# Hybrid attention block: stationary q and k weights, a product on GpSimd and later value matmuls in the stick-breaking groups

## Chip, cores, metric

One core of a Trainium2 chip. The metric is the time of one execution on the device in microseconds; the kernel before has a median of 2731.22 us over 3 runs (2727.44 to 2734.09). The profile is of one further execution, 2740.3 us.

## The reference

Sequence 2048, width 1024, one layer; all in float32.

```python
u = rms_norm(h, norm1_w)
dq, dk, dv, sq, sk, sv = split(u @ w_in)
# A: differential attention, 4 heads: two softmax maps per head, T5 bias, chunk-causal
attn = softmax(q0 k0 + bias) - lam * softmax(q1 k1 + bias);  y_A = rms_norm(attn @ v)
# B: stick-breaking attention, 8 heads of 64, strictly causal
z = einsum('bqhd,bkhd->bhqk', q, k) * scale
log_1mb = where(mask, log_sigmoid(-z), 0)
rem = cumsum(log_1mb, reverse=True) - log_1mb
a = where(mask, exp(log_sigmoid(z) + rem), 0);  y_B = rms_norm(a @ v)
h = h + concat(y_A, y_B) @ w_out
h = h + (silu(u2 @ w_gate) * (u2 @ w_up)) @ w_down      # u2 = rms_norm(h, norm2_w)
```

Part B is computed without logarithms: `a` is the sigmoid of z times the running product, from the right, of the sigmoids of -z.

## The kernel before

**Precision.** TensorE multiplies float16. Each operand is split into a high and a low half, and a product is made of three (or all four) of the half products.

**Groups.** The attention runs in 8 groups `g`: groups 0 to 3 are one differential head each (`diff_attn`), 4 to 7 are two stick-breaking heads each (`sb_attn`, head index `m`). A group has three parts.

- *Projection* (`proj`, 16 token tiles of 128). `proj_tile` (L320) keeps a tile of u, 128 x 128, in the array and streams 384 weight columns (q, k, v) past it, 24 matmuls per tile, into one of two PSUM buffers `pj` (pool `psj`). `proj_out` splits q, k into the staging tile `st` and v into `v` (`split_psum`, L327 to L330: the high half by ACT or DVE as `pick` finds by a running load account, the low half by DVE). After four tiles `proj_batch` has SP transpose q and k by DMA (L372) and swap the halves of q by two copies (L374). The tiles of u are loaded for every group (L386). The projection of a group is issued during the group before.
- *Scores to weights* (`stage_a`). For each block of 128 queries `i`, each block `b` of 1024 keys from the right and each head `m`, chunks of up to 512 keys: two score matmuls (L448) into one of four PSUM buffers `sc`; ACT takes sigmoid(-z) to the tile `om` (L554) and sigmoid(z) in place (L555); DVE scans `om` with a running product (L557) and multiplies (L558) into `be`. `be` and `om` are `z4` tiles, 9 buffers. Then `split_t`: ACT casts `be` to float16 (L89) into an `s16` tile (3 buffers), POOL subtracts for the low half (L98), SP transposes the pair by DMA into `aT` (L403, 6 buffers).
- *Values* (`stage_b`, L458): `aT` is the stationary operand, v streams, three matmuls of 64 columns per 128 keys, into the PSUM tile `yp`. It runs `PD` = 5 items behind `stage_a`; at the end of a group a loop drains the rest. After four query blocks `finish` normalises, transposes and stores to `ms`.

`diff_attn` has the same build with softmax (L483 to L507) and with values two query blocks behind.

**Order.** The program is issued once per item and a scheduler orders the instructions of each engine ahead of time on a modelled timeline, by priority and readiness; on the chip every engine takes its queue in that order. During group 7 the output projection (L761) begins; then follows the feed-forward part, where TensorE is busy nearly throughout.

Of the kernel before, what the change touches and what calls it, by code (L numbers as in the profile page):

```python
# [11 lines left out]
F32 = mybir.dt.float32  # L12
# [47 lines left out]
def block(tc, a, out):  # L60
# [3 lines left out]
    with top:  # L64
# [62 lines left out]
        DVE.memset(mhalf[:], -0.5)  # L127

# [122 lines left out]
        with ExitStack() as ph1:  # L251
# [71 lines left out]

            def split_psum(hi, lo, src, n):
# [21 lines left out]

            @pri("pb")
            def proj_batch(g, G, B):
                st, v, raw = B
                qT = sp.tile([P, 4, 4, P], F16, tag="qT", bufs=QB, name=nm("qT"))  # L350
                kT = sp.tile([P, 2, 4, P], F16, tag="kT", bufs=KB, name=nm("kT"))
# [27 lines left out]
            def proj(g, G, fresh=None):  # L379
                for t in range(NT):  # L380
# [6 lines left out]
                    if t % 4 == 0:  # L387
                        st = pp.tile([P, 4, 4, 2, 64], F16, tag="st", name=nm("st"))
                        v = sp.tile([P, 4, 256], F16, tag="v", bufs=KB, name=nm("v"))
                        raw = pp.tile([P, 4, 256], F32, tag="raw", name=nm("raw")) if g < 4 else None  # L390
# [7 lines left out]
            def split_t(src, n, he="ADP", le="DP"):  # L398
                s16 = s16p.tile([P, 2048], F16, tag="s16", bufs=SB, name=nm("s16"))
                to16(s16[:, :n], src, n, he)  # L400
                tt(s16[:, n : 2 * n], src, s16[:, :n], ALU.subtract, n, le)
                aT = sp.tile([P, 16, P], F16, tag="aT", bufs=AB, name=nm("aT"))
# [37 lines left out]

            def fq(g, i):
                k = 2 if g == NG - 1 else 4
                return (i % k, k)

            @pri("sc")
            def score_chunk(G, sc, i, q, m, w, cut=False):
                for o in range(2):
                    PE.matmul(sc[:, : 128 * w].rearrange("p (t n) -> p t n", n=P), lhsT=G["q"][i // 4][:, 2 - 2 * o + m, i % 4, :], rhs=G["k"][q][:, m, 0:w, :], start=o == 0, stop=o == 1)  # L448
                if cut:
                    PE.matmul(sc[:, 128 * w - P : 128 * w], lhsT=idb[:], rhs=tri[:], start=False, stop=True, skip_group_check=True)  # L450
# [9 lines left out]
            def diff_attn(g, G):  # L460
                @pri("at")
                def probs(i):
# [8 lines left out]
                    for m in range(2):  # L471
                        nx = 0
                        for b in range(nb):
                            n = min(1024, L - 1024 * b)
                            z = z4()
                            for c in range((n + 511) // 512):
                                lo, hi = 512 * c, min(512 * c + 512, n)
                                sc = ps.tile([P, 512], F32, tag="sc", bufs=4, name=nm("sc"))
                                score_chunk(G, sc, i, 2 * b + c, m, (hi - lo) // P)
# [35 lines left out]
                def values(i, aTs, ssum):  # L515
                    r, k = fq(g, i)
# [8 lines left out]
                held = []  # L525
                for i in range(NT):
                    if i % 4 == 0:
                        level()
                    held.append((i, probs(i), sums[0]))
                    if len(held) > 2:  # L530
                        values(*held.pop(0))
                    yield ((i + 1) * (i + 2) / 2 + CD * (i + 1)) / (136 + 16 * CD), i + 1
                for u in held:
                    values(*u)

            def sb_attn(g, G):
                last = {}

# [689 lines left out]
```

## Time and profile before

| | |
|---|---|
| median of 3 runs | 2731.22 us |
| profiled execution | 2740.3 us |
| its span, first to last instruction | 2738.5 us |
| busy, share of the span: PE, DVE, POOL, ACT | 91%, 72%, 52%, 49% |
| mean granted TensorE clock | 0.967 |
| first scan of group 4, of group 5, of group 6, of group 7 | 606, 794, 965, 1127 us |

The row of a window gives the busy time of each engine in that stretch. A row of a group of instructions gives line, engine, operation, tiles with their shapes and the count; then busy time in us and the mean of one in ns; then the idle time of the engine in front of them and what ended most of it. Durations of matmuls overlap one another, since the array is pipelined: what a matmul costs in a dense stream is read from the difference of two bursts, not from the mean.

### The profile page before, as it was taken

What the parts mean: (1) busy time and instruction counts of PE and PEld (TensorE: products, weight loads), DVE (VectorE), ACT (ScalarE), POOL (GpSimd) and SP (SyncE); (2) the same over time, 40 slices, a digit from 0 to 9 for tenths busy, and PEclk for the clock granted to TensorE, in tenths of its full rate; (3) what the DMA queues carried; (4) which work ended last, traced back from release to release, by engine and by line L of the source; (5) the groups of instructions that cost most, each with busy time, mean ns of one, the idle gap of its engine ahead of it and who ended that gap; (6) DMA issues with size and microseconds to landing.
All of it is one profiled execution on the core that took longest, in us unless ns stands there. A gap on an engine that the chain in (4) does not pass through costs nothing.

```text
span 2738.5 us, 45414 instructions
## 1 busy us (share of the span) xinstructions
PE 2490.0 (91%) x17084; PEld 1409.8 (51%) x17084; DVE 1978.5 (72%) x3752; ACT 1353.3 (49%) x2539; POOL 1429.8 (52%) x1002
## 2 busy tenths in 40 slices
PE   7998989898978886889989898999999999999999
PEld 4655656565545553457775444444444444444444
DVE  6888879888888989987766777777786544434434
ACT  4665656566868778765644534344342212121121
POOL 2577677765554545546655566565664332222322
PEclk9999999998999997899999999999999999999999
DMA  6788787789998997997896665566657845635532
GB/s 227 199 164 178 151 198 164 180 171 200 208 201 184 212 186 151 203 192 208 213 289 256 220 234 191 208 221 216 231 204 283 316 158 181 220 128 193 192 116 93
DMA packets 646830, 543.52 MB, mean 198 GB/s; under 512 B 506369, under 2 KB 573953, under 8 KB 636369
## 3 DMA queue, kind: packets, MB, share of 16 engines
q1 hardware_dynamic: 644784, 538.53, 71.8%
q8 instruction: 134, 2.20, 0.3%
q0 software_dynamic: 512, 1.36, 0.2%
q10 hardware_dynamic: 1312, 0.72, 0.1%
q14 instruction: 88, 0.71, 0.1%
HBM read 261.08 MB, written 147.32 MB: 149 GB/s over the span
## 4 chain that ended last, share of the span: by engine, by line
PE 36%; DVE 9%; DMA 4%; POOL 3%; issue 3%; ACT 2%; SPq 0%; DVEq 0%; POOLq 0%; ACTq 0%
PE pd L1034 14%; PE pm L934 7%; PE pd L934 5%; PE pa L934 5%; DVE wd L215 2%; PE po L761 2%; DMA stages<-in_w_down_dram 1%; POOL stages L98 1%; DVE wu L215 1%; DMA aT<-s 1%; DVE z L557 1%; DVE cg L999 1%; DVE cg L98 1%; POOL s L98 1%; PE pj L320 1%
## 5 line engine op out<-in xcount | busy, mean ns | idle before, releaser
L98 POOL TENSOR_TENSOR s<-z,s 128x1024 f16<-128x1024 f32 (+7 forms) x288 | 474.4, 1655 | 320.1 <-ACT s L89 281.4
L320 PE MATMUL pj<-w,xt 128*128 128x384 f16 x3072 | 577.0, 336 | 19.2 <-DMA xt<-xs 5.6
L320 PEld LDWEIGHTS <-xt 128*128 128x128 f16 x3072 | 301.5, 101 | 233.1 <-issue 36.1
L557 DVE TENSOR_TENSOR_SCAN z<-z,sc 128x512 f32<-128x512 f32 (+3 forms) x320 | 356.1, 1114 | 72.1 <-ACT sc L555 68.8
L448 PE MATMUL sc<-kT,qT 128*128 128x512 f16 (+3 forms) x1280 | 348.3, 364 | 59.4 <-DVE z L558 23.7
L1034 PE MATMUL pd<-wd,act 128*128 128x512 f16 x1764 | 394.0, 381 | 7.2 <-DVE cu L968 7.1
L458 PE MATMUL yp<-v,aT 128*128 128x64 f16 (+1 forms) x4896 | 281.5, 209 | 82.3 <-DMA aT<-s 81.7
L458 PEld LDWEIGHTS <-aT 128*128 128x128 f16 x4896 | 245.4, 102 | 172.1 <-DMA aT<-s 110.4
L934 PEld LDWEIGHTS <-wg 128*128 128x128 f16 x1848 | 181.8, 98 | 228.1 <-issue 14.6
L934 PEld LDWEIGHTS <-wu 128*128 128x128 f16 x1848 | 180.8, 98 | 216.5 <-issue 2.0
L98 POOL TENSOR_TENSOR act<-cg,act 128x512 f16<-128x512 f32 x109 | 149.8, 1385 | 262.3 <-ACT act L993 262.3
L1034 PEld LDWEIGHTS <-act 128*128 128x128 f16 x1764 | 173.0, 98 | 216.6 <-issue 10.2
L89 ACT CAST s<-z 128x128 f16<-128x128 f32 (+7 forms) x216 | 170.3, 790 | 154.8 <-DMA aT<-s 72.9
L98 POOL TENSOR_TENSOR stages<-stages 128x512 f32<-128x512 f32 x97 | 172.9, 1783 | 120.1 <-DVE wg L215 41.4
L98 POOL TENSOR_TENSOR hs<-hs,cu 128x512 f32<-128x512 f32 x102 | 132.6, 1306 | 165.6 <-DVE hs L1040 62.7
L554 ACT ACTIVATE z<-sc,c 128x512 f32<-128x512 f32 (+3 forms) x320 | 204.4, 639 | 23.7 <-PE sc L448 18.9
L558 DVE TENSOR_TENSOR z<-sc,z 128x512 f32<-128x512 f32 (+3 forms) x320 | 193.7, 606 | 8.5
L555 ACT ACTIVATE sc<-sc,c 128x512 f32<-128x512 f32 (+3 forms) x320 | 196.5, 614 | 0.0
L1040 DVE SCALAR_TENSOR_TENSOR hs<-pd,c,hs 128x512 f32<-128x512 f32 x144 | 106.5, 748 | 118.5 <-PE pd L1034 113.6
L761 PE MATMUL po<-wo,mt 128*128 128x256 f16 x1536 | 180.7, 275 | 12.3 <-DVE xf L764 6.8
L993 ACT CAST act<-cg 128x512 f16<-128x512 f32 x126 | 76.9, 616 | 231.4 <-DVE cg L999 192.7
L934 PE MATMUL pm<-X,wu 128*128 128x512 f16 x792 | 179.1, 379 | 1.8 <-ACT cg L979 1.7
(241 smaller groups left out, 4109.1 us busy)
## 6 DMA issues: line engine op xcount, KB each, us to landing
xt<-xs SPq DMA_DIRECT2D x112, 512.0 KB, 4.4
hs<-hd SPq DMA_DIRECT2D x72, 512.0 KB, 4.5
hd<-hs SPq DMA_DIRECT2D x56, 512.0 KB, 5.8
split<-wg SPq DMA_DIRECT2D x11, 1792.0 KB, 6.9
split<-wu SPq DMA_DIRECT2D x11, 1792.0 KB, 6.7
split<-wd SPq DMA_DIRECT2D x11, 1792.0 KB, 6.8
wg<-split SPq DMA_DIRECT2D x11, 1792.0 KB, 7.4
wd<-split SPq DMA_DIRECT2D x11, 1792.0 KB, 9.1
```

What stands on the lines that cost most here:

```text
L89: ACT.copy(dst, src)
L98: (DVE if e == "D" else POOL).tensor_tensor(dst, a_, b_, op)
L320: PE.matmul(pj[:, :384], lhsT=xv[:, xi, kt, :], rhs=G["w"][:, wi, kt, :], start=n == 0, stop=n == 23)
L448: PE.matmul(sc[:, : 128 * w].rearrange("p (t n) -> p t n", n=P), lhsT=G["q"][i // 4][:, 2 - 2 * o + m, i % 4, :], rhs=G["k"][q][:, m, 0:w, ...
L458: PE.matmul(yp[:, y0 : y0 + wd], lhsT=aT[:, a_, :], rhs=v[:, v_ : v_ + wd], start=start and j == 0 and q == 0, stop=stop and j == nb - 1 a ...
L554: ACT.activation(om[:, lo:hi], sc[:, :w], AF.Sigmoid, scale=G["nkz"][:])
L555: ACT.activation(sc[:, :w], sc[:, :w], AF.Sigmoid, scale=G["kz"][:])
L557: DVE.tensor_tensor_scan(ov, ov, sc[:, :w], om[:, hi : hi + 1], op0=ALU.mult, op1=ALU.bypass)
L558: DVE.tensor_tensor(be[:, lo:hi], sc[:, :w], om[:, lo + 1 : hi + 1], ALU.mult)
L761: PE.matmul(po[:, sl], lhsT=mt[:, kt, P * xi : P * xi + P], rhs=wos[2 * h + n][wi][:, kt, :], start=q == 0, stop=q == 23)
L934: PE.matmul(ps_[:].rearrange("p (t n) -> p t n", n=P), lhsT=wv[:, wo, wi, 128 * kt : 128 * kt + 128], rhs=X[xo][:, :, xi, kt, :], start=st ...
L1034: PE.matmul(po[:], lhsT=act[:, ao, xi, 128 * j : 128 * j + 128], rhs=W["d"][:, wo, wi, :], start=start and u == 0 and q == 0, stop=u == nu ...
```

## The change

`turned(g)` holds for groups 4, 5 and 6. In these the weights of q and k are the stationary operand and 128 tokens stream, so q and k come out of PSUM already transposed; v is computed as before, 128 columns at a time. Two tiles share two PSUM buffers, one for q and k, one for v. The transposes and swaps by DMA fall away. q is stored per head, with the other head's 64 rows set to zero by a mask (`half`), and scores take three matmuls: high x high, low x high, high x low. Of each item's chunks those with c = 1 ("aside") write the second sigmoid to SBUF, and their product is POOL's.

For all groups, value matmuls are ordered on PE behind the last score matmul issued before them (`issue_after`), and one list `late` carries pending values from one group to the next. In groups 4 and 5 values run 7 items behind in place of 5, and two further buffers each for `s16` and `aT` come from tiles that lie idle there (`raw`, `st`).

```diff
+            def turned(g):
+                return 4 <= g < NG - 1
+
+            @pri("pm")
+            def proj_turned(G, xt, pq, pv, r):
+                xv = xt[:].rearrange("p (s k n) -> p s k n", s=2, k=KT)
+                for c in range(3):
+                    n = 0
+                    for kt in range(KT):
+                        for xi, wi in ((0, 0), (0, 1), (1, 0)):
+                            w_, x_ = G["w"][:, wi, kt, 128 * c : 128 * c + 128], xv[:, xi, kt, :]
+                            o = pv[:, P * r : P * r + P] if c == 2 else pq[:, 256 * c + P * r : 256 * c + P * r + P]
+                            PE.matmul(o, lhsT=x_ if c == 2 else w_, rhs=w_ if c == 2 else x_, start=n == 0, stop=n == 23)
+                            n += 1
+
+            @pri("po")
+            def turned_out(pq, pv, qT, kT, v, j):
+                two = slice(j - 1, j + 1)
+                q2, k2 = (pq[:, 256 * c : 256 * c + 256].rearrange("p (t n) -> p t n", t=2) for c in range(2))
+                for m in range(2):
+                    ACT.mul(qT[:, m, two, :], q2, half[:, m : m + 1])
+                    DVE.scalar_tensor_tensor(qT[:, 2 + m, two, :], q2, half[:, m : m + 1], qT[:, m, two, :], op0=ALU.mult, op1=ALU.subtract)
+                note("A", 800)
+                note("D", 800)
+                split_psum(kT[:, 0, two, :], kT[:, 1, two, :], k2, 256)
+                vv = v[:, two, :].rearrange("p t (h s e) -> p t h s e", h=2, s=2)
+                split_psum(vv[:, :, :, 0, :], vv[:, :, :, 1, :], pv[:, :256].rearrange("p (t h e) -> p t h e", t=2, h=2), 256)
...
+                    if turned(g):
...
+                        if t % 2 == 0:
+                            pq, pv_ = (psj.tile([P, 512], F32, tag="pj", name=nm("pj")) for _ in range(2))
+                        proj_turned(G, xt, pq, pv_, t % 2)
+                        if t % 2 == 1:
+                            turned_out(pq, pv_, qT, kT, v, t % 4)
...
-            def split_t(src, n, he="ADP", le="DP"):
-                s16 = s16p.tile([P, 2048], F16, tag="s16", bufs=SB, name=nm("s16"))
+            def split_t(src, n, he="ADP", le="DP", wide=None):
+                if wide is not None and wide % 5 in (1, 3):
+                    s16 = pp.tile([P, 4, 256], F32, tag="raw", name=nm("s16"))[:].rearrange("p t n -> p (t n)").bitcast(F16)
+                else:
+                    s16 = s16p.tile([P, 2048], F16, tag="s16", bufs=SB, name=nm("s16"))
...
+                if wide is not None and wide % 4 == 3:
+                    aT = pp.tile([P, 4, 4, 2, 64], F16, tag="st", name=nm("aT"))[:].rearrange("p c t s e -> p (c t) (s e)")
...
+            front, late = [], []
+
+            def behind(n):
+                while len(late) > n:
+                    late.pop(0)()
...
-            def score_chunk(G, sc, i, q, m, w, cut=False):
-                for o in range(2):
-                    PE.matmul(sc[:, : 128 * w].rearrange("p (t n) -> p t n", n=P), lhsT=G["q"][i // 4][:, 2 - 2 * o + m, i % 4, :], rhs=G["k"][q][:, m, 0:w, :], start=o == 0, stop=o == 1)
+            def score_chunk(G, sc, i, q, m, w, cut=False, turned=False):
+                terms = ((m, 0), (2 + m, 0), (m, 1)) if turned else ((2 + m, m), (m, m))
+                for o, (a_, b_) in enumerate(terms):
+                    last = PE.matmul(sc[:, : 128 * w].rearrange("p (t n) -> p t n", n=P), lhsT=G["q"][i // 4][:, a_, i % 4, :], rhs=G["k"][q][:, b_, 0:w, :], start=o == 0, stop=o == len(terms) - 1)
...
                 def values(i, aTs, ssum):
+                    with tc.issue_after(front[-1]):
+                        values_now(i, aTs, ssum)
...
+                    late.append(functools.partial(values, i, probs(i), sums[0]))
+                    behind(2)
...
+                lag = PD + 2 if g < NG - 2 else PD
...
-                        score_chunk(G, sc, i, 2 * b + c, m, w // P, b == i // 8 and hi == n)
+                        front.append(score_chunk(G, sc, i, 2 * b + c, m, w // P, b == i // 8 and hi == n, turned(g)))
+                        aside = c == 1 and turned(g)
+                        beta = be[:, lo:hi] if aside else sc[:, :w]
                         ACT.activation(om[:, lo:hi], sc[:, :w], AF.Sigmoid, scale=G["nkz"][:])
-                        ACT.activation(sc[:, :w], sc[:, :w], AF.Sigmoid, scale=G["kz"][:])
+                        ACT.activation(beta, sc[:, :w], AF.Sigmoid, scale=G["kz"][:])
                         ov = om[:, lo:hi][:, ::-1]
                         DVE.tensor_tensor_scan(ov, ov, sc[:, :w], om[:, hi : hi + 1], op0=ALU.mult, op1=ALU.bypass)
-                        DVE.tensor_tensor(be[:, lo:hi], sc[:, :w], om[:, lo + 1 : hi + 1], ALU.mult)
+                        (POOL if aside else DVE).tensor_tensor(be[:, lo:hi], beta, om[:, lo + 1 : hi + 1], ALU.mult)
...
+                            late.append(functools.partial(stage_b, i, m, b, n, aT))
+                            behind(lag)
...
-                for u in pend:
-                    stage_b(*u)
+                if g == NG - 1:
+                    behind(0)
```

50 lines of the change are left out of this document (32 added, 18 removed).

## The prediction

> **What bounds the kernel now.** I read the stages first: busy time per engine between the first scan of one group and the first scan of the next (columns: window, length, PE, PEld, DVE, ACT, POOL busy, granted clock, DMA share, GB/s). Groups 4, 5 and 6 are the windows that begin at 605, 794 and 965; 150:600 is three of the differential groups, 470:605 the last of them, 1127:1384 group 7.
>
> ```profile
> span 2738.5 us, 45414 instructions
> ...
> 150.00:600.00 450.00, 407.66 (x3279) 263.15 (x3280) 388.89 (x1142) 270.30 (x707) 322.14 (x226) 0.98 0.80 172
> ...
> 470.00:605.00 135.00, 121.40 (x974) 77.91 (x972) 118.83 (x345) 79.78 (x208) 90.96 (x66) 0.97 0.78 169
> 605.00:794.00 189.00, 162.97 (x1614) 103.51 (x1612) 167.12 (x313) 147.21 (x289) 103.03 (x63) 0.94 1.02 207
> 794.00:965.00 171.00, 140.20 (x1420) 86.83 (x1418) 151.78 (x268) 133.61 (x252) 86.20 (x54) 0.91 0.99 195
> 965.00:1127.00 162.00, 123.71 (x1299) 76.04 (x1296) 149.52 (x251) 131.17 (x246) 83.86 (x55) 0.85 0.87 173
> 1127.00:1384.00 257.00, 223.72 (x2289) 172.01 (x2290) 199.51 (x344) 166.08 (x308) 144.96 (x103) 0.96 0.87 205
> ```
>
> Groups 4 to 6 take 522 us. DVE is busy for 468 of them (90%), ACT for 412 (79%), POOL for 273 (52%). DVE leads; its idle time is 54 us. Next, the groups of instructions in 605:1127, and who waited for whom there:
>
> ```profile
> L557 DVE TENSOR_TENSOR_SCAN z<-z,sc 128x512 f32<-128x512 f32 (+3 forms) x240 | 266.9, 1113 | 40.6 <-ACT sc L555 38.0
> L98 POOL TENSOR_TENSOR s<-z,s 128x1024 f16<-128x1024 f32 (+7 forms) x147 | 237.8, 1625 | 229.8 <-ACT s L89 217.1 <-issue 6.3 <-DVE st L330 3.4
> L320 PE MATMUL pj<-w,xt 128*128 128x384 f16 x1166 | 220.2, 339 | 5.4 <-DMA xt<-xs 2.8 <-DVE st L330 1.9 <-DVE m L178 0.7
> L554 ACT ACTIVATE z<-sc,c 128x512 f32<-128x512 f32 (+3 forms) x241 | 153.4, 636 | 14.8 <-PE sc L448 10.2 <-PE sc L450 2.8 <-POOL s L98 1.7
> L555 ACT ACTIVATE sc<-sc,c 128x512 f32<-128x512 f32 (+3 forms) x241 | 147.3, 611 | 0.0
> L558 DVE TENSOR_TENSOR z<-sc,z 128x512 f32<-128x512 f32 (+3 forms) x240 | 145.2, 607 | 6.6
> L448 PE MATMUL sc<-kT,qT 128*128 128x512 f16 (+3 forms) x482 | 139.8, 379 | 42.4 <-DVE z L558 18.3 <-DVE z L545 13.6 <-DVE z L547 8.7
> L458 PE MATMUL yp<-v,aT 128*128 128x64 f16 (+1 forms) x2524 | 123.5, 204 | 45.0 <-DMA aT<-s 44.8
> L89 ACT CAST s<-z 128x1024 f16<-128x1024 f32 (+7 forms) x144 | 115.8, 805 | 77.8 <-DMA aT<-s 44.0 <-DVE z L558 11.7 <-issue 11.5
> ...
> L330 DVE SCALAR_TENSOR_TENSOR st<-pj,st 128x256 f16<-128x256 f32 x49 | 19.8, 407 | 2.1 <-ACT st L327 2.1
> ...
> L327 ACT ACTIVATE st<-pj 128x256 f16<-128x256 f32 x49 | 19.1, 396 | 10.5 <-DVE v L330 10.5
> L327 ACT ACTIVATE v<-pj 128x128 f16<-128x128 f32 x49 | 14.2, 297 | 1.2 <-PE pj L320 1.1
> L330 DVE SCALAR_TENSOR_TENSOR v<-pj,v 128x128 f16<-128x128 f32 x49 | 13.1, 273 | 0.1
> L215 DVE SCALAR_TENSOR_TENSOR w<-wst,sW,w 128x1536 f16<-128x1536 f32 x6 | 12.6, 2110 | 0.0
> ```
>
> The scan and the product behind it are 412 of DVE's 468 us. Of DVE's idle time 38 us are waits of the scan for ACT. ACT in turn lost 44 us in front of its cast (L89): the cast needs a free s16 buffer, which a transposing DMA still reads. The timeline at the seam of groups 4 and 5 shows the chain: ACT stands 2.5 us and 2.0 us at casts, the sigmoids queue behind, and DVE's scan comes 4.55 us late:
>
> ```profile
> 798.95 0.30 ACT L89 CAST s<-z 128x128 f16<-128x128 f32 x1 [2.52 <-DMA aT<-s]
> ...
> 801.25 0.30 ACT L89 CAST s<-z 128x128 f16<-128x128 f32 x1 [2.00 <-DMA aT<-s]
> ...
> 802.29 0.75 DVE L557 TENSOR_TENSOR_SCAN z<-z,sc 128x256 f32<-128x256 f32 x1 [4.55 <-ACT sc L555]
> ```
>
> PE's own 45 us of waits for aT cost little by themselves: the scores wait for DVE as well (42 us), so PE has room.
>
> **The product on GpSimd.** A group has 32 chunks with c = 1 (in i from 4 to 15, both heads), 96 in all: 60 of 512 columns, 12 each of 384, 256 and 128, together 39,936 columns. From the start of a product to the next scan:
>
> ```profile
> 1101.92 0.69 DVE L558 TENSOR_TENSOR z<-sc,z 128x512 f32<-128x512 f32 x1
> ...
> 1102.53 1.27 DVE L557 TENSOR_TENSOR_SCAN z<-z,sc 128x512 f32<-128x512 f32 x1
> ```
>
> That is 0.61 us per 512 columns, so DVE is rid of 39,936/512 x 0.61 = 48 us. POOL's price for a float32 product in SBUF isn't in this stage. The nearest rows, of the whole trace:
>
> ```profile
> L98 POOL TENSOR_TENSOR stages<-stages 128x512 f32<-128x512 f32 x97 | 172.9, 1783 | 120.1 <-DVE wg L215 41.4 <-DVE wd L215 34.1 <-DVE wu L215 31.0
> L98 POOL TENSOR_TENSOR hs<-hs,cu 128x512 f32<-128x512 f32 x102 | 132.6, 1306 | 165.6 <-DVE hs L1040 62.7 <-DVE cu L1040 45.4 <-issue 44.8
> ```
>
> The first is strided, the second contiguous like ours, so I take 1.31 us (bounds 1.31 and 1.78): 78 x 1.31 = 102 us, POOL 273 to 375. ACT writes the second sigmoid to SBUF (636 ns against 611): 96 x 0.025 = 2 us.
>
> Row L215 reads two SBUF operands on DVE and takes 2110 ns. [...]
>
> **The projection.** Before, two token tiles cost DVE 2 x (407 + 273) ns and ACT 2 x (396 + 297). After, the pair has four high halves and four low ones of 256 columns; the lows are DVE's, two highs (q) are ACT's, and of the 48 highs for k and v the compiled order gives DVE 35. DVE: 4 x 0.407 + 35/24 x 0.40 = 2.21 against 1.36, so +0.85 us a pair, 24 pairs, +20 us. A group's projection runs during the group before: 7 us fall into group 3, 14 into groups 4 and 5. ACT gains some 0.4 us a pair.
>
> PE's pitch, from differences of bursts in the timeline, and from a dense stretch of the last phase (234 matmuls of 512 in 50 us):
>
> ```profile
> 66.72 3.58 PE L320 MATMUL pj<-w,xt 128*128 128x384 f16 x21
> ...
> 79.74 1.63 PE L320 MATMUL pj<-w,xt 128*128 128x384 f16 x9
> ...
> 167.07 0.94 PE L458 MATMUL yp<-v,aT 128*128 128x128 f16 x14
> ...
> 168.84 0.67 PE L458 MATMUL yp<-v,aT 128*128 128x128 f16 x9
> ...
> 2150.00:2200.00 50.00, 50.00 (x234) 22.62 (x233) 23.79 (x33) 9.36 (x15) 13.10 (x10) 1.00 0.70 262
> ```
>
> 384 columns: (3.58 - 1.63)/12 = 163 ns. 128 columns with a weight load each: (0.94 - 0.67)/5 = 54 ns, three of them 162. The projection costs PE nothing more. The bursts' raw quotient is 74 ns, the upper bound.
>
> **The scores.** A third matmul per chunk: 240 chunks of 435 columns on average, 435/512 x 0.214 = 0.182 us each, +44 us for PE. What PE can carry beside a busy DVE is seen in the differential groups (150:600, PE alone):
>
> ```profile
> L320 PE MATMUL pj<-w,xt 128*128 128x384 f16 x1225 | 225.2, 328 | 6.2 <-ACT raw L341 5.0 <-DMA xt<-xs 1.1
> L448 PE MATMUL sc<-kT,qT 128*128 128x512 f16 (+3 forms) x560 | 146.5, 356 | 8.8 <-DVE z L483 3.2 <-DVE mx L487 1.8 <-DMA kT<-st 1.5
> L458 PE MATMUL yp<-v,aT 128*128 128x128 f16 x1434 | 114.7, 224 | 25.4 <-DMA aT<-s 25.3
> ```
>
> By pitches that is 1225 x 0.163 + 560 x 0.182 + 1434 x 0.054 = 379 us in 450, 84%, with DVE at 86% and POOL at 72%. In groups 4 to 6 it is 1166 x 0.163 + 482 x 0.182 + 2524 x 0.027 (the 512 pitch scaled to 64) = 346 us, 66% of 522 (more at the granted clock of 0.85 to 0.94). With 390 in 488 us it would be 80%: near the other stage's share, below it. The scores run up to four PSUM buffers ahead of DVE, which covers a late one.
>
> **Transposes, buffers, order.** The 16 transposes and 16 half swaps of groups 5 and 6 leave the queue of SP, and 8 of each of group 4 before it:
>
> ```profile
> L372 SPq DMA_TRANSPOSE qT<-st x32: 1232/1266/2467, 71.7 to 1207.6; - x32
> ...
> L374 SPq DMA_DIRECT2D qT<-qT x64: 467/586/1172, 75.8 to 1216.8; - x64
> ```
>
> That is 24 x 1.27 + 24 x 0.59 = 45 us of issue less in the queue that also issues the aT transposes; worth nothing by itself, it makes s16 free sooner. Two more s16 and two more aT buffers (groups 4 and 5) aim at the 44 us of casts. Values behind later scores is an order within PE's queue: behind a value wait projections and later values, and the aT buffer is released later. In the compiled order a value stands 13 chunks behind its scores in groups 4 and 5 (before 9.5), 10 in group 6 (9), 9 in group 7 (7), and as before in groups 0 to 3, so I expect PE's 45 us of aT waits nearly gone and nothing there for the differential groups. Carrying values over seams changes little: the order before already had 8 to 10 chunks of the next group in front of a group's last values.
>
> **The sum.** DVE in groups 4 to 6: 468 - 48 + 14 = 434. I keep its idle time at 54: the s16 stalls should shrink, but PE (80%), ACT (83%) and POOL (77%) come close and will bring waits of their own. 434 + 54 = 488, -34 us. Group 3, with DVE at 88%: +5 of its 7. Group 7: -3, from PE's deeper order. In all -32: 2738.5 - 32 = 2706.5 us of span, and on the profiled execution's 2740.3 us it is 2708. That execution lay 9 us above the median, 2731.2; so 2699. Own range: idle time 25 lower or 20 higher, 2674 to 2720.
>
> **Rivals.**
> - *The idle time goes too.* The 38 us of scans waiting for ACT vanish with the s16 stalls: -32 - 30, 2669. For it: the 4.55 us at the seam were such a stall. Against: group 6 gets no buffers. 0.13.
> - *POOL's product comes late* (slower). It may stand behind a subtraction (1625 ns mean) and takes 1.31, while the chunk c = 0 gives it only 1.27 + 0.61; the cast of the item waits for it, and ACT is in order. Up to 1 us a chunk: 96 us. It decides from 34/96 = 0.35 us a chunk on. At 0.6 us: +58, 2757. Against: POOL has 23% to spare, and the compiled order leaves a later chunk's sigmoids between. 0.13.
> - *PE becomes the bound* (slower). One pair of tiles holds both PSUM buffers of the projection, so PE stands at the next pair until ACT and DVE have emptied them, at least 2 x 0.396 + 2 x 0.407 = 1.6 us for 16 pairs, and each may queue behind a scan and a product more, 3.5 us, 56 us in all; and the short matmuls may run at 74 ns, 2304 x 20 ns = 46 us. It decides where PE's 390 us and these losses exceed 84% of 522, 438 us: from 48 us on. With both, 492/0.84 = 586, +64, is the end; half of that, +32 with groups 3 and 7 at +2, gives 2765. [...] 0.10.
> - *It does nothing.* The bound is the loop through ACT, SP and DMA, whose share is 0.87 to 1.02, and DVE's saved time turns idle: about -5, 2726. 0.10.
> - The forecast: 0.54.
>
> **Chances.** 0.2%, about what a measurement of this kernel can tell, is 5.5 us. Faster: 0.54 + 0.13 + half of the last rival, 0.72; same 0.05; slower 0.23. The range for 8 in 10 takes in the first rival and reaches to the first of the two slower ones: 2667 to 2757.
>
> **What would show it.** Right: from the first scan of group 4 to that of group 7 near 488 us, DVE busy near 434, POOL near 375; L558's successor on DVE at 144 instead of 240; casts hardly waiting for aT in groups 4 and 5; PE's aT waits under 10 us; 128-wide projections at 54 ns. Wrong: casts waiting for POOL's product, PE waiting for ACT or DVE at the first matmul of a pair, or DVE's idle time over 88 us.

## The result, and the profile after

The changed kernel is slower: median 2745.89 us over 7 runs (2738.67 to 2747.91) against 2733.37 us (2727.44 to 2736.76, 7 runs), ratio 1.0044, 95% interval 1.0033 to 1.0055. The forecast was 2699 us, a gain. All medians are of fast executions; one of 5470.6 us among the eight of before_same_priority, a kernel of the experiments, is left out. The profiled execution took 2743.9 us, 3.6 us more than that of before; the medians differ by 12.5 us, since the profiled execution of before lay above its median, as the prediction noted. So the stages below explain 3.6 us of profile; what the other 9 us consist of no profile shows.

The stages of the changed kernel, cut at the first scans of groups 4 to 7 as before (columns: window, length, PE, PEld, DVE, ACT, POOL busy, granted clock, DMA share, GB/s):

```profile
606.00:767.00 161.00, 137.40 (x2088) 110.38 (x2086) 148.97 (x251) 139.19 (x260) 123.32 (x93) 0.97 0.93 182
767.00:940.00 173.00, 145.97 (x2263) 118.18 (x2261) 144.44 (x251) 133.66 (x240) 114.81 (x87) 0.97 0.82 168
940.00:1122.00 182.00, 156.62 (x2137) 118.93 (x2132) 151.78 (x271) 132.64 (x242) 120.54 (x90) 0.97 0.85 180
1122.00:1390.00 268.00, 231.05 (x2369) 178.94 (x2369) 201.92 (x353) 163.62 (x301) 145.22 (x101) 0.96 0.80 201
```

Group 4 became 26 us shorter (187.5 to 161), group 5 stayed (172 and 172), group 6 became 20 us longer (162 to 182): together 515.6 us in place of 521.1. Group 7, which the change leaves alone apart from the order of its values, became 12 us longer (256.5 to 268.6, to the end of the last scan). What precedes differs by 0.2 us, and what follows is 3 us shorter. DVE is busy for 445 us of groups 4 to 6 (before 467) and idle for 70 (before 54): some 16 of the 22 us that DVE was spared came back as idle time.

The groups of instructions in 606:1122 of the changed kernel:

```profile
L626 DVE TENSOR_TENSOR_SCAN z<-z,sc 128x512 f32<-128x512 f32 (+3 forms) x241 | 265.8, 1110 | 49.8 <-ACT sc L624 28.6 <-ACT z L624 13.8 <-PE sc L514 0.5
...
L512 PE MATMUL sc<-kT,qT 128*128 128x512 f16 (+2 forms) x718 | 174.4, 357 | 53.3 <-DVE kT L362 14.4 <-DVE z L627 12.9 <-DVE z L612 11.4
L623 ACT ACTIVATE z<-sc,c 128x512 f32<-128x512 f32 (+2 forms) x241 | 165.2, 690 | 25.9 <-PE sc L514 13.5 <-PE sc L512 12.3
L341 PE MATMUL pj<-xt,w 128*128 128x128 f16 x1937 | 151.0, 222 | 9.8 <-DVE v L363 8.8 <-PE sc L514 0.5 <-DVE m L183 0.4
...
L523 PE MATMUL yp<-v,aT 128*128 128x64 f16 (+1 forms) x2496 | 122.1, 197 | 6.8 <-DMA aT<-s 6.8
L89 ACT CAST s<-z 128x1024 f16<-128x1024 f32 (+7 forms) x143 | 121.6, 854 | 67.8 <-DMA aT<-s 16.4 <-POOL s L98 14.7 <-DVE z L627 14.1
...
L627 POOL TENSOR_TENSOR z<-z,z 128x512 f32<-128x512 f32 (+3 forms) x96 | 92.5, 964 | 90.3 <-DVE z L626 83.8 <-DVE z L612 3.0 <-DVE c L176 1.7
...
L627 DVE TENSOR_TENSOR z<-sc,z 128x512 f32<-128x512 f32 (+3 forms) x144 | 88.5, 617 | 4.0
...
L349 ACT ACTIVATE qT<-pj,half 128x256 f16<-128x256 f32 x42 | 22.9, 545 | 7.4 <-DVE qT L350 7.0 <-PE pj L341 0.2
...
L350 DVE SCALAR_TENSOR_TENSOR qT<-pj,half,qT 128x256 f16<-128x256 f32 x42 | 19.7, 469 | 4.0 <-ACT qT L349 4.0
...
L220 DVE SCALAR_TENSOR_TENSOR w<-wst,sW,w 128x1536 f16<-128x1536 f32 x6 | 14.4, 2408 | 0.5 <-POOL w L219 0.5
```

Read from the top: the scan still waits for ACT, 42 us in two entries of its row (before 38). ACT, which waited 13 us for PE in front of the sigmoids before, now waits 26 (L623). PE in turn waits where it hardly did (1 us, for the swap of q's halves): 14.4 us of the scores' idle time end with `kT` (L362), the high half of k, written by DVE. Four waits make up nearly all of it. The views of who waited for whom in 767:940 and in 940:1122 (total us, times, longest) have:

```profile
PE sc L512 <- DVE kT L362: 5.0, 2, 4.6
```
```profile
PE sc L512 <- DVE kT L362: 9.4, 3, 4.2
```

The waits that the change aimed at are mostly gone: the casts' for aT from 44 to 16 us, the values' for aT from 45 to 7.

TensorE's queue, in which the trace has every matmul, says why k is late. In the compiled order of before, the projection of group 5 begins behind 35 of the 80 chunks of group 4 and ends behind the 20th of group 5; in that of the changed kernel it begins behind the 61st and ends behind the 57th of group 5. Group 6 is like it (59 and 53, before 20 and 13); group 7's projection begins later (55, before 14) and ends alike (28 and 30). It is not the last tiles of k that come too late: these are needed from the 65th chunk on. Tiles 4 and 5 are needed from the 9th chunk on, 6 and 7 from the 17th, 8 and 9 from the 25th, 10 and 11 from the 37th; and in groups 5 and 6 of the changed kernel each of these four pairs ends directly in front of that chunk, which leaves no time for its evacuation. The four waits stand at such places: 4.6 us behind the 8th chunk of group 5, and 2.5, 2.7 and 4.2 us behind the 8th, 16th and 24th of group 6. The projection's matmuls have a low priority (-200) in both kernels; in the changed one they slip until they are just in time.

### The profile page after: what moved, and what is told of

It reads as the page before. It is cut to its first block, busy times and chain, and to the rows that moved or that the text cites. A ratio compares the mean times of both kernels' runs of the same rounds, so it can differ in the third digit from the quotient of the medians.

```text
span 2742.1 us, 50494 instructions
## 1 busy us (share of the span) xinstructions
PE 2509.9 (92%) x19628; PEld 1506.2 (55%) x19628; DVE 1955.7 (71%) x3711; ACT 1346.8 (49%) x2488; POOL 1516.2 (55%) x1097
## 5 line engine op out<-in xcount | busy, mean ns | idle before, releaser
L512 PE MATMUL sc<-kT,qT 128*128 128x512 f16 (+3 forms) x1520 | 380.9, 353 | 76.5 <-DVE z L627 17.8
L325 PE MATMUL pj<-w,xt 128*128 128x384 f16 x1920 | 358.6, 335 | 14.2 <-ACT raw L374 4.3
L523 PE MATMUL yp<-v,aT 128*128 128x64 f16 (+1 forms) x4896 | 273.8, 204 | 31.8 <-DMA aT<-s 31.0
L325 PEld LDWEIGHTS <-xt 128*128 128x128 f16 x1920 | 188.6, 100 | 144.6 <-issue 25.6
L623 ACT ACTIVATE z<-sc,c 128x512 f32<-128x512 f32 (+3 forms) x320 | 215.5, 677 | 27.8 <-PE sc L514 14.1
L512 PEld LDWEIGHTS <-qT 128*128 128x128 f16 x1520 | 128.9, 99 | 151.2 <-issue 33.0
L341 PE MATMUL pj<-xt,w 128*128 128x128 f16 x2304 | 178.3, 222 | 9.8 <-DVE v L363 8.8
L1007 PE MATMUL pm<-X,wg 128*128 128x512 f16 x792 | 181.3, 382 | 1.9 <-ACT bx L1182 1.9
```

Source lines behind the costliest of these rows:

```text
L325: PE.matmul(pj[:, :384], lhsT=xv[:, xi, kt, :], rhs=G["w"][:, wi, kt, :], start=n == 0, stop=n == 23)
L341: PE.matmul(o, lhsT=x_ if c == 2 else w_, rhs=w_ if c == 2 else x_, start=n == 0, stop=n == 23)
L512: last = PE.matmul(sc[:, : 128 * w].rearrange("p (t n) -> p t n", n=P), lhsT=G["q"][i // 4][:, a_, i % 4, :], rhs=G["k"][q][:, b_, 0:w, :] ...
L523: PE.matmul(yp[:, y0 : y0 + wd], lhsT=aT[:, a_, :], rhs=v[:, v_ : v_ + wd], start=start and j == 0 and q == 0, stop=stop and j == nb - 1 a ...
L623: ACT.activation(om[:, lo:hi], sc[:, :w], AF.Sigmoid, scale=G["nkz"][:])
L1007: PE.matmul(ps_[:].rearrange("p (t n) -> p t n", n=P), lhsT=wv[:, wo, wi, 128 * kt : 128 * kt + 128], rhs=X[xo][:, :, xi, kt, :], start=st ...
```

## Experiments

All differences are to medians of before on the same chip. A row is sure to some 3 to 5 us to either side by its interval, and the difference of two rows to little better than 5 us; it also compares kernels from different chips, by way of before. For groups 4 to 6 the table gives the first scan of group 4 to that of group 7, and for group 7 the first scan to the end of the last; both are of one profiled execution. Against before, profiles and medians disagree by up to 10 us (product_on_pool_alone is 7.9 us faster in the profiles, 1.9 slower by medians), so a few us of a stage prove nothing.

| kernel | us to before | ratio, 95% interval | groups 4-6 | group 7 |
|---|---|---|---|---|
| before (profile) | | | 521.1 | 256.5 |
| changed | +12.5 | 1.0044 [1.0033, 1.0055] | 515.6 | 268.6 |
| two_terms | -23.1 | 0.9917 [0.9903, 0.9930] | 499.4 | 253.8 |
| product_on_dve | +26.0 | 1.0091 [1.0078, 1.0103] | 541.8 | 254.6 |
| no_order | -2.6 | 0.9992 [0.9979, 1.0005] | 515.1 | 264.0 |
| proj_same_priority | -16.2 | 0.9937 [0.9925, 0.9950] | 498.4 | 251.7 |
| before_same_priority | +9.7 | 1.0038 [1.0023, 1.0052] | 513.0 | 263.4 |
| two_terms_same_priority | -31.9 | 0.9883 [0.9864, 0.9902] | 479.8 | 252.3 |
| same_priority_no_order | -21.3 | 0.9924 [0.9907, 0.9942] | 489.8 | 261.2 |
| product_on_pool_alone | +1.9 | 1.0005 [0.9993, 1.0017] | 506.7 | 268.6 |
| turned_projection_alone | +1.6 | 1.0011 [1.0001, 1.0021] | 522.8 | 253.7 |
| order_alone | -6.9 | 0.9976 [0.9964, 0.9987] | 515.5 | 255.1 |
| product_and_order | -13.2 | 0.9957 [0.9942, 0.9973] | 497.2 | 260.8 |
| no_wide_buffers | -11.9 | 0.9962 [0.9948, 0.9976] | 506.9 | 252.0 |
| wide_buffers_lag5 | -6.9 | 0.9980 [0.9968, 0.9991] | 508.9 | 259.7 |
| no_wide_no_order | +0.6 | 1.0007 [0.9997, 1.0017] | 510.2 | 266.9 |
| no_wide_late_priority | -0.8 | 0.9997 [0.9986, 1.0008] | 497.7 | 269.5 |
| late_priority_no_order | -14.4 | 0.9948 [0.9933, 0.9963] | 498.4 | 259.4 |
| after_weights_later | +8.8 | 1.0035 [1.0017, 1.0052] | 520.8 | 264.4 |
| best_weights_later | -21.2 | 0.9925 [0.9911, 0.9939] | 481.6 | 269.4 |

### The suspects: third matmul, GpSimd's product, the order, the priority

```diff
# two_terms
-                terms = ((m, 0), (2 + m, 0), (m, 1)) if turned else ((2 + m, m), (m, m))
+                terms = ((m, 0), (2 + m, 0)) if turned else ((2 + m, m), (m, m))
```

> The changed kernel with the third score matmul (q high x k low) left out in groups 4 to 6: its scores lack that term, PE has 44 us less work, DVE, ACT and POOL have the same. If PE's added work is what ate the gain (theory A: PE is full, the projection slips to the seams of the groups and DVE starves there), the time falls by 25 to 40 us against the changed kernel, to about 2710 us, and DVE's idle time in groups 4 to 6 falls from 70 to about 45 us. If POOL's late product (theory B) or the order of the values (theory C) is the cause, it falls by under 10 us, to about 2738 us.

35.6 us below the changed kernel (12.5 + 23.1), as expected of the theory that PE's added work ate the gain; the idle time fell less far than to the 45 us expected. In its row of groups 4 to 6 DVE has the same work (444 us) and 15 us less idle time:

```profile
605.00:1104.00 499.00, 413.68 (x6305) 337.29 (x6302) 443.69 (x780) 405.09 (x740) 363.94 (x269) 0.94 0.92 188
```

So the third matmul, costed at nothing, is the dearest part. By the profiles 16 us of it lie in groups 4 to 6, 15 in group 7, where scores have two matmuls in both kernels. In the compiled order of two_terms the pairs of groups 5 and 6 from tile 4 on end 9 to 17 chunks before they are needed, and the scores' wait for `kT` and `qT` is 1 us. But most of the delay is there without the third matmul too: the projection of group 5 begins behind the 48th chunk of group 4 and ends behind the 47th of group 5, against 35 and 20 before.

```diff
# product_on_dve
-                        aside = c == 1 and turned(g)
+                        aside = False
```

> The changed kernel with the product of all chunks on DVE again and the second sigmoid in PSUM. Theory B (POOL's product comes late and holds up the casts): no slower than the changed kernel, 2735 to 2746 us, although DVE has 48 us more. Theories A and C: DVE was relieved in earnest, so at least part of the 48 us comes back: 2755 to 2785 us.

13.5 us slower than the changed kernel. GpSimd's product is no net loss there; the rival that it comes late falls, as far as it would have decided the result.

```diff
# no_order
-                    with tc.issue_after(front[-1]):
-                        stage_c(i, m, b, n, aT)
+                    stage_c(i, m, b, n, aT)
```

> The changed kernel without the order of values behind later scores; the list that is carried over the seams, the deeper lag and the buffers stay. Theory C (PE stands at scores that wait for DVE while ready values queue behind them, and group 7 starts later): faster by 8 to 20 us, 2726 to 2738 us. Theory A: within 5 us of the changed kernel; theory B: the same.

15.1 us below the changed kernel (the same edit was made for the differential groups' values). PE's waits for aT are back, and yet it is faster:

```profile
L512 PE MATMUL sc<-kT,qT 128*128 128x512 f16 (+3 forms) x722 | 172.6, 353 | 12.6 <-DVE z L626 4.8 <-DVE z L613 3.0 <-DVE z L611 2.5
...
L523 PE MATMUL yp<-v,aT 128*128 128x64 f16 (+1 forms) x2522 | 121.9, 196 | 53.1 <-DMA aT<-s 52.6
```

Sparing those waits by this order did not pay here. The scores' wait for k is gone as well (0.4 us), although pairs of k still end directly in front of the chunks that need them (the 16th and 24th in both groups); but groups 4 to 6 are as long as in the changed kernel (515.1 and 515.6). So the 14 us of waits for k are not by themselves what the stage loses.

```diff
# proj_same_priority (PRI)
-"pm": -200
+"pm": 0
```

> The changed kernel with the projection's matmuls at the same priority as the scores in the schedule (PRI pm 0 in place of -200), in all groups. Theory A: the projections no longer slip to the seams, DVE's idle time there goes, 10 to 25 us faster in groups 4 to 7, against which scores are issued later everywhere: 2720 to 2745 us. Theories B and C: no gain, 2745 to 2770 us.

28.7 us below the changed kernel, with the same work. The waits named above shrink, each in its row:

```profile
L626 DVE TENSOR_TENSOR_SCAN z<-z,sc 128x512 f32<-128x512 f32 (+3 forms) x241 | 265.3, 1109 | 39.5 <-ACT sc L624 24.4 <-ACT z L624 9.0
...
L512 PE MATMUL sc<-kT,qT 128*128 128x512 f16 (+1 forms) x717 | 175.6, 353 | 53.6 <-DVE z L626 20.5 <-DVE z L627 14.2 <-DVE z L612 9.2
L623 ACT ACTIVATE z<-sc,c 128x512 f32<-128x512 f32 (+2 forms) x241 | 159.4, 666 | 8.8 <-PE sc L512 4.2 <-PE sc L514 3.5 <-DVE wo L220 0.9
L341 PE MATMUL pj<-xt,w 128*128 128x128 f16 x1951 | 136.5, 221 | 1.7 <-DVE m L183 1.2 <-DVE v L363 0.5
```

The scan waits 33 us for ACT in place of 42. Of the scores' idle time 4 us still end with `kT` (the rest waits for DVE, as before the change), and ACT waits 8 us for PE in place of 26.

### Is it the slip, or is TensorE full?

```diff
# before_same_priority: the kernel before with "pm": 0
# two_terms_same_priority: two_terms with "pm": 0
# same_priority_no_order: no_order with "pm": 0
```

> The kernel before, with the projection's matmuls at the same priority as the rest; nothing else. If the gain of 26 us that the same edit gave in the changed kernel comes from the third score matmul having pushed the projection to the ends of the groups, there is nothing to push back here: within 4 us of the kernel before (2732 to 2740). If the low priority was a fault of the kernel in any case, it gains here too, about 15 us: 2720.

> The changed kernel with two score matmuls in place of three (the product of q's high and k's low half is left out, so the result is less exact) and the projection at the same priority. If the third matmul hurts only because the projection slips behind it, then with the projection kept in its place it costs next to nothing: 2712 to 2720, within 7 us of the three-term kernel at the same priority. If PE itself is full in groups 4 to 6, the 44 us of matmuls cost their price whatever the order: 2690 to 2700, 20 us or more below it.

> The changed kernel with the projection at the same priority and without the order of values behind later scores. If the two losses are separate they add up: 2719.75 - 12.5 = 2707. If the order hurts because the values that it holds back push the projection further, the priority has cured that already: 2717 to 2722.

The kernel before loses 9.7 us by this edit, which neither theory allowed, though 8 us of its groups 4 to 6 are gained: its first group-4 scan comes 8 us later (614.0 against 606.1) and group 7 takes 7 us more. With the priority equal the third matmul still costs 15.7 us (-16.2 to -31.9), between the two expectations and all in groups 4 to 6 (498.4 to 479.8). So both hold in part: some 16 us go with the third matmul in groups 4 to 6 at either priority; the other 20 come only with the low priority, and 15 of them lie in group 7. Without the order the equal priority gives -21.3: the fastest version with all terms, 34 us below the changed kernel and 21 below the kernel before, again between the two expectations.

### Each part alone

```diff
# product_on_pool_alone: the kernel before, and in stage_a (with its entry in the load account)
+                        aside = c == 1 and 4 <= g < NG - 1
# turned_projection_alone: the changed kernel without order, further buffers, deeper lag, carrying
-                        aside = c == 1 and turned(g)
+                        aside = False
# order_alone: the changed kernel with lag = PD, no further buffers, and
-                return 4 <= g < NG - 1
+                return False
```

> The kernel before, with the product of the chunks c = 1 of groups 4 to 6 on GpSimd; nothing else of the change. Without the third matmul PE has room. If DVE bounds groups 4 to 6 in the kernel before, as the prediction had it, its 48 us come off nearly whole: 2695 to 2705. If the idle time of DVE grows by most of it (casts that wait for aT buffers, POOL), as in the changed kernel, where the product earned 16: 2715 to 2722.

> The kernel before with stationary q and k weights in groups 4 to 6 and the three score matmuls that this takes; the product stays on VectorE, no further buffers, no order, values drained at the end of each group. If TensorE's further matmuls push the projection to the ends of the groups, as they did in the changed kernel, slower by 15 to 30 us: 2750 to 2765. If the transposes by DMA that fall away were what the casts waited for, this pays for the matmuls: 2725 to 2738.

> The kernel before with value matmuls behind the last score matmul issued and pending values carried over the seams; the projection, the product and the buffers as before. If the order costs by itself, as its removal from the changed kernel gained 12.5 us: about 2745. If it costs only beside the third score matmul, where TensorE has less room: within 5 us of the kernel before, 2729 to 2739; the prediction had taken it for a gain (TensorE's 45 us of waits for aT gone).

The product alone earns nothing (+1.9, slower than either expectation), where the forecast's logic gives 48. Its rows in groups 4 to 6:

```profile
603.00:1109.00 506.00, 413.09 (x4265) 259.12 (x4263) 435.15 (x797) 394.64 (x715) 353.81 (x264) 0.94 0.98 196
```
```profile
L559 DVE TENSOR_TENSOR_SCAN z<-z,sc 128x512 f32<-128x512 f32 (+3 forms) x240 | 265.9, 1114 | 48.0 <-ACT sc L557 36.2 <-ACT z L557 5.9 <-PE sc L448 0.5
...
L89 ACT CAST s<-z 128x1024 f16<-128x1024 f32 (+7 forms) x144 | 117.1, 819 | 84.7 <-DMA aT<-s 60.3 <-DVE z L560 6.0 <-DVE z L545 5.8
...
L329 DVE TENSOR_SCALAR v<-pj 128x128 f16<-128x128 f32 x44 | 12.2, 279 | 6.8 <-PE pj L320 5.8 <-PE yp L458 1.0
L329 DVE TENSOR_SCALAR st<-pj 128x256 f16<-128x256 f32 x26 | 10.8, 414 | 0.0
```

DVE's products fall by 57 us, but its busy time by 32 only (467 to 435): the load account saw an emptier DVE and gave it 70 high halves, 23 us, of the 98 that ACT wrote before. DVE's idle time rises from 54 to 71 us, with the casts waiting 60 us for aT (before 44). What is left in the profile, 14 us in groups 4 to 6, goes in group 7 (+12).

The turned projection alone, with its third matmul, is worth nothing (+1.6, as the second expectation had it); which of its parts pays for which was not separated. It is also the control for the slip:

```profile
600.00:1123.00 523.00, 453.60 (x6589) 355.34 (x6587) 479.74 (x826) 420.25 (x785) 271.85 (x173) 0.96 0.84 176
```
```profile
L512 PE MATMUL sc<-kT,qT 128*128 128x512 f16 (+3 forms) x722 | 176.9, 356 | 35.7 <-DVE z L627 19.6 <-DVE z L612 9.0 <-DVE z L614 4.5
```

Its projections end as late as in the changed kernel (behind the 53rd and 59th chunk), and yet the scores wait only 2 us for k, and DVE's idle time is 43 us, less than before. So a late projection does not cost by itself; it does so in company.

The order alone, with the carrying over the seams, gains 6.9, more than expected, and its values wait 18 us for aT in place of 45.

### Which part turns it

```diff
# no_wide_buffers: the changed kernel with
+                lag = PD
+                    return n, split_t(be[:, :n], n, "A", "P", None)
# wide_buffers_lag5: with lag = PD alone
# no_wide_no_order: no_wide_buffers and no_order
# product_and_order: order_alone and product_on_pool_alone
```

> The changed kernel without the two further buffers for s16 and aT and with values 5 items behind in groups 4 and 5. If these groups are full for TensorE, buffers that spare waits of ACT earn little: within 5 us of the changed kernel, 2741 to 2751. If the loop through cast, transpose and aT was what bounded the kernel before, as product_on_pool_alone suggests, the waits of the casts come back: 2755 to 2770.

> The changed kernel with the further s16 and aT buffers, but with values 5 items behind in groups 4 and 5 as in the kernel before. If the deeper lag cost the 25 us: 2718 to 2724. If the buffers did: 2740 to 2750.

> The changed kernel without the further buffers and the deeper lag, and without the order of values: what is left is the turned projection with three score matmuls, the product on GpSimd, and pending values carried over the seams. If the order helps when the buffers are few, as it did alone: 2725 to 2732, some 7 us above no_wide_buffers. If it costs beside the third matmul: about 2708.

> The kernel before with the product on GpSimd and the order of values with carrying over the seams; projection, scores and buffers as before, so two score matmuls, exact as before. If the parts add up (+2 and -7): 2726 to 2730. If the product earns once TensorE's waits for aT are gone, as it earned 16 in the changed kernel: 2708 to 2715, the best that computes everything by the old projection.

All four results lie outside what was expected of them, those of product_and_order and wide_buffers_lag5 between their two expectations. Without further buffers and lag the change is 11.9 us faster than before. The deeper lag costs 19.4 us (-6.9 to +12.5); the buffers cost 5 (-11.9 to -6.9), which is within the noise. Rows of no_wide_buffers in groups 4 to 6:

```profile
L512 PE MATMUL sc<-kT,qT 128*128 128x512 f16 (+2 forms) x719 | 174.3, 356 | 22.0 <-DVE z L627 6.6 <-DVE z L612 5.2 <-DVE z L626 3.9
...
L89 ACT CAST s<-z 128x1024 f16<-128x1024 f32 (+7 forms) x144 | 118.7, 829 | 70.5 <-DMA aT<-s 35.0 <-DVE z L627 15.5 <-issue 8.0
```

The casts wait 35 us for aT, twice as long as in the changed kernel, and the whole is faster: here too the waits that were spared were not what the stage ended on. The wait for `kT` and `qT` is 2 us.

The order gains 12.5 us without the further buffers and lag (+0.6 to -11.9) and, with the carrying, 15.1 on top of the product alone (+1.9 to -13.2), and costs 15.1 with buffers and lag (-2.6 to +12.5). Its sign hangs on the rest.

```diff
# no_wide_late_priority: no_wide_buffers, and for the projections of groups 4 to 7 only
+"pt": 0
# late_priority_no_order: no_order with the same
```

> The changed kernel without the further buffers and the deeper lag, and with the projection of groups 4 to 7 at the same priority. If both edits cure the same slip of the projection, the second adds little to the first (2720.4): 2712 to 2720. If the two losses are separate, the gains add up (25.5 + 26 below the changed kernel): 2694 to 2702.

> The changed kernel without the order of values behind later scores, and with the projection at the same priority for groups 4 to 7 alone; groups 0 to 3 keep the low one. With the priority everywhere the first scans of the first differential group came 3 to 5 us later than in the changed kernel. If that loss is carried to the end, this is 4 to 5 us better than the same priority everywhere without the order: 2707. If it is made good by group 4 (where the first scan stood at 605.6 against 606.3), it is the same: 2711 to 2713.

Both misses. Equal priority on top of no_wide_buffers shortens groups 4 to 6 by 9 us (506.9 to 497.7), but the time before group 4 grows by 9.5 (618.3 against 608.8) and group 7 by 17.5, of which what follows gives back 8: 11 us slower by the medians. So the 28.7 us in the changed kernel, where the edit was made for all groups, are not the priority's own price; they fit the view that it undoes what order and lag did there. Keeping groups 0 to 3 at the low priority without the order gives no more than the priority everywhere (-14.4 against -21.3).

### Group 7

Between these kernels group 7 takes 252 to 270 us; it computes the same in all. In the changed kernel the loss arises in the first chunks: the eighth chunk after its first starts 31 us after it, before 24, and by the 16th all but 1 of the 12 us are lost. The timeline there (start, duration, engine, line, idle time in front):

```profile
1134.73 2.22 POOL L219 TENSOR_SCALAR wo<-z,sW 128x1024 f16<-128x1024 f32 x2 [0.28 <-DVE sW L204]
1135.95 2.07 DVE L220 SCALAR_TENSOR_TENSOR wo<-z,sW,wo 128x1024 f16<-128x1024 f32 x1
1136.09 1.63 PE L325 MATMUL pj<-w,xt 128*128 128x384 f16 x9
1139.66 1.25 DVE L220 SCALAR_TENSOR_TENSOR wo<-z,sW,wo 128x1024 f16<-128x1024 f32 x1
1141.39 5.74 PE L325 MATMUL pj<-w,xt 128*128 128x384 f16 x24 [3.67 <-DVE st L363]
1141.92 0.62 ACT L89 CAST s<-z 128x512 f16<-128x512 f32 x1 [4.72 <-POOL s L98]
1147.16 0.28 ACT L360 ACTIVATE v<-pj 128x128 f16<-128x128 f32 x1 [4.63 <-PE pj L325]
1147.47 0.29 DVE L363 SCALAR_TENSOR_TENSOR v<-pj,v 128x128 f16<-128x128 f32 x1 [3.84 <-ACT v L360]
```
```profile
1141.00:1147.00 6.00, 5.61 (x25) 3.05 (x26) 2.60 (x8) 0.62 (x1) 2.08 (x2) 0.72 1.12 213
```

Halves of the output weights (`wo`) stand ahead of evacuations on DVE and of subtractions on POOL; ACT waits 4.7 us for POOL, PE 3.7 us for a projection buffer, and then PE's 24 matmuls take 5.74 us where 163 ns each makes 3.9: the granted clock was 0.72 in these 6 us. ACT and DVE wait for them in turn. Within the burst, behind the 3.67 us in which PE stood, the granted clock was 0.52 in 1141.4:1144.8 and 0.97 in 1144.8:1147.1; weight loads start 0.32 us apart from 1141.88 to 1144.76, and the last twelve take 1.97 us, 164 ns each. The clock is not what makes group 7 longer, though: over the group's first 60 us its mean is 0.91 (1122:1182), before 0.89 (1127:1187). To see whether the place of the weights decides:

```diff
# after_weights_later: the changed kernel; best_weights_later: same_priority_no_order
-WT = (4, 7, 10)
+WT = (6, 9, 12)
```

> The changed kernel with the preparation of the first three quarters of the output weights two projection tiles later in group 7 (tiles 6, 9, 12 in place of 4, 7, 10). Groups 4 to 6 keep their order and their 515 us. If group 7's 12 us come from the collision at its seam (VectorE, GpSimd and ScalarE in turn behind the preparation, then TensorE), group 7 falls to 252 to 260 us: 2730 to 2738 in all. If they come from the projection of group 7 being late, nothing changes: 2742 to 2750.

> The fastest full version so far (same priority for the projection, no order of values, 2712; its group 7 takes 261 us) with the same shift. If the seam is a matter of place, group 7 may fall to 252: 2703. If the shift only shuffles the order: 2708 to 2722.

It doesn't: +8.8 in place of +12.5, the intervals overlap, and group 7 still takes 264 us. The wait of 3.67 us is gone there, but PE waits 3.0 and 3.1 us at 54 and 57 us into the group instead. In best_weights_later groups 4 to 6 gained 8 us and group 7 lost 8. What makes group 7 long or short is open.

## Why the prediction was wrong

A gain of 32 us was forecast, and the time rose by 12.5; "slower" had a chance of 0.23. That 2746 us lies inside the range of 2667 to 2757 is luck: the range was stretched to the first of two slower rivals, and neither of them happened as described. The signs of being wrong that were named stayed small too: casts waited 18 us for POOL (15 of them for its subtraction), PE 9 us at the pairs, and DVE's idle time stayed under 88 us.

**What failed first: the third score matmul, "+44 us for PE", put at nothing in the sum.** It was compared with a stage in which PE reached 84%, and 80% looked like room. By the same pitches PE's work in groups 4 to 6 of the changed kernel is 384 us of 516 (2945 x 0.054 + 163 x 0.163 + 718 x 0.182 + 2496 x 0.027), 74%, and yet it cost: how busy PE is on average doesn't say where its free time lies. The measured price is 35.6 us in the changed kernel, 15.7 with the projection at equal priority. The rival "PE becomes the bound" had the right engine, but neither of its two losses came: the pairs' wait for their buffers is 8.8 us (bounded at 56), and a dense stretch keeps the short pitch:

```profile
652.36 2.67 PE L341 MATMUL pj<-xt,w 128*128 128x128 f16 x45 [0.38 <-DVE m L183]
...
704.95 2.18 PE L341 MATMUL pj<-xt,w 128*128 128x128 f16 x36
```

(2.67 - 2.18)/9 = 54 ns, as forecast. What the runs show in place of nothing: some 16 us in groups 4 to 6 at either priority, and some 20 more that go when the projection is given another place in the queue, which no item of the sum covered. How the 16 us arise inside the stage, and why 15 of the 20 lie in group 7, is open.

**"I keep its idle time at 54."** It became 70; in kernels of the table it is 56 without the third matmul and 53 with equal priority (length of the stage less DVE's busy time). These 16 us and DVE's 445 in place of 434 make the stage 516 in place of 488.

**DVE's busy time.** GpSimd took 96 products as forecast and needed 92.5 us (forecast 102). That DVE came to 445 us in place of 434 can be told apart by two kernels. The projection by itself adds 12 us (479.7 in turned_projection_alone, 467.4 before), where the working has 24 x 0.27 = 6 for the low halves; the evacuations of q took 469 ns in place of 407, and 21 of the 24 pairs fell into groups 4 to 6. The product takes away 36 net (480.9 in product_on_dve, 445.2 in the changed kernel), because the load account then hands DVE high halves of k and v, which in product_on_dve are ACT's:

```profile
L362 DVE TENSOR_SCALAR kT<-pj 128x256 f16<-128x256 f32 x20 | 8.3, 413 | 0.0
L362 DVE TENSOR_SCALAR v<-pj 128x256 f16<-128x256 f32 (+1 forms) x21 | 7.8, 371 | 0.3 <-PE pj L341 0.2
```

The forecast had these, with 14 us, a third of them in group 3; all 16 fell into groups 4 to 6. Row L220 (L215 before), which reads two SBUF operands on DVE, has a mean of 2408 ns in place of 2110, and 2086 in product_on_dve, but 2571 in order_alone, where GpSimd has no product; so the runs don't show that the product adds to it, and the row's six are under 2 us longer in all. Scan and product on DVE kept their times (1110 and 617 ns, before 1113 and 607; at 512 columns 1273 and 683, before 1274 and 686).

**That DVE bounds the stage.** Only partly: sparing DVE 32 us net gave 14 us in groups 4 to 6 and nothing in the end (product_on_pool_alone); in the changed kernel the product is worth 13.5. The rival "it does nothing" named this, with the loop through ACT, SP and DMA: the casts' wait for aT rose from 44 to 60 us there.

**Buffers and order.** Both did what was said of them (casts' waits 44 to 16, PE's 45 to 7), and neither paid in the changed kernel; the order alone, in the kernel before, gains 6.9. The forecast took the deeper lag for harmless; it costs 19.4 us. Order, lag, buffers and low priority make one knot: in the changed kernel, taking out any one of them gains 15.1, 19.4 (lag alone), 24.4 (lag and buffers) or 28.7 us, and these don't add up (no order and no further buffers together: 12). In each of these four the scores' wait for k and q is 4 us or less. But only the equal priority moves the projection forward in the compiled order (group 6's ends behind the 48th chunk; without the order or the buffers behind the 57th, no earlier than in the changed kernel, the 53rd), so how the other three avoid the wait stays open, and no_order shows that its end alone does not shorten groups 4 to 6.

**Group 7: "-3".** It was +12, and decided the sign in the profile. Its cause is not settled; it comes in kernels without the third matmul too (product_on_pool_alone, 268.6).

## What to carry to other kernels

Before work is added to an engine on the ground of its average load, look where in its queue the low-priority work stands and who needs it first: here the filler slipped until it was just in time, and some of its consumers waited. A wait that a row shows has no known worth until a kernel without it is faster; here 38 us of PE's waits were removed at a loss. And where edits interact through a compiled order, each one alone and each one left out can differ in sign, so a decision needs the combination itself: here equal priority and no order on top of the change, 2712.0 us.

## What the runs showed of the hardware

ACT's sigmoids were slower in the kernels in which GpSimd multiplied, most of all in the changed one, though they are the same instructions; by form, in 606:1121, first product_on_dve, then the changed kernel:

```profile
L623 ACT ACTIVATE z<-sc,c 128x512 f32<-128x512 f32 x159 | 112.1, 705 | 10.9 <-PE sc L512 10.7
L624 ACT ACTIVATE sc<-sc,c 128x512 f32<-128x512 f32 x159 | 108.5, 682 | 0.0
```
```profile
L623 ACT ACTIVATE z<-sc,c 128x512 f32<-128x512 f32 x168 | 128.0, 768 | 8.4 <-PE sc L512 7.8 <-PE sc L514 0.6
L624 ACT ACTIVATE sc<-sc,c 128x512 f32<-128x512 f32 x108 | 80.1, 742 | 0.0
```

9% for the sigmoid of 512 columns. The mean of the first of a chunk (L623; L554 before) at 512 columns is 703 ns in the kernel before, 705 with three matmuls and no product (product_on_dve), 719 and 727 with the product and two matmuls (product_on_pool_alone, two_terms) and 768 in the changed kernel. Over all widths of groups 4 to 6 it is 637 ns before and in order_alone and 641 in product_on_dve, 652 to 666 in product_on_pool_alone, two_terms, no_wide_buffers and proj_same_priority, and 690 in the changed kernel. What slows them was not tried. And evacuations of q, which ACT and DVE read from one PSUM tile in turn, took 545 and 469 ns, where 256 columns cost 396 and 407 before; these have a further operand (`half`) and a transposed target, so the cause is open.

The granted clock of PE rose from 0.94, 0.91 and 0.85 in groups 4, 5 and 6 to 0.97 in each. PE's busy share went from 86, 82 and 76% to 85, 84 and 86%, so the share alone does not tell the clock.
